# Layer 0's first shift and scale: the sums over the condition as column-packed TensorE matmuls

## The chip, the core and the metric

The kernel runs on one core of a Trainium2 chip. The core has a matrix engine (TensorE, "PE" in the profile, with its weight loads as "PEld"), a vector engine (VectorE, DVE), a scalar engine (ScalarE, ACT), GpSimd (POOL), and SyncE (SP), whose queue issues most of the DMA transfers here. TensorE writes its results into PSUM, eight banks of 128 partitions by 512 float32; everything else lies in SBUF, 128 partitions wide. Every engine works through its own queue, whose order is fixed when the kernel is built; an instruction waits there until its data have come and its buffer is free. The metric is the device time of one execution in microseconds (us); the medians of several executions are compared.

## The reference

A trunk of two layers over 256 positions of 2048 channels. What the change touches is the modulation at the head of layer 0: a condition vector `c` of 2048 elements, passed through SiLU, is multiplied with a 2048 x 12288 matrix, which gives six vectors of 2048; the first two, shift and scale, are applied to the normalised input before its projection.

```python
c_act = jax.nn.silu(c)
for l in range(DEPTH):
    mod = (c_act @ w_mod[l] + b_mod[l]).reshape(bn, 6, d)
    shift_m, scale_m, gate_m = mod[:, 0, None], mod[:, 1, None], mod[:, 2, None]
    shift_f, scale_f, gate_f = mod[:, 3, None], mod[:, 4, None], mod[:, 5, None]
    h = layer_norm(x) * (1.0 + scale_m) + shift_m
    proj = h @ w_in[l]
    ...                      # four mixers on parts of proj, concatenated
    x = layer_norm(ALPHA * x + (1.0 + gate_m) * (y @ w_out[l]), ...)
    h = layer_norm(x) * (1.0 + scale_f) + shift_f
    x = layer_norm(ALPHA * x + (1.0 + gate_f) * conv_ffn(h, ...), ...)
```

So each element of shift and scale is a dot product of 2048 terms, and all weights of the product (33.5 MB for these two vectors) are used only once.

## The kernel before

Channels are cut into 16 k-tiles of 128 (`KT`), positions into two tiles of 128. Layer 0's input projection can't start before shift and scale are there for the channels that it contracts over, so both are done in five pieces of k-tiles, `PIECES` (line 45): two, two, four, four and four k-tiles. Function `by_pieces` (in `mixers`' layer-0 case) runs over the pieces: while the products of piece q's projection run, the modulation weights of piece q+1 are loaded and summed. For every piece the projection has four parts: D (1024 columns), U, V and E (512 each), all with `mm` (line 79).

- **D** is contracted in TensorE with plain float32 operands for the first four k-tiles (`D_c<-hF,wexact` in the profile) and after that with pairs of rounded halves, `hi` and `lo`, of weights and activations (`D_c<-hT,whi`, `D_c<-hT,wlo`). The weights are split by ScalarE (line 460) and VectorE (line 461), the activations by lines 479 and 480.
- **U, V, E** are contracted with plain float32 operands (`U<-hF,wexact`, `V<-wexact,hF`, `E<-hF,wexact`). Their partial sums of a piece are copied by ScalarE out of PSUM (lines 1259 and 1264) and added by VectorE (lines 1261, 1265).

Within a piece, `by_pieces` writes the program in four steps: a quarter of D's products, then one of U, V, E; after the fourth quarter of D comes the next piece. In each step a share of the next piece's modulation units (`some_mods`) is put ahead of the products, and ahead of the last quarter of D comes `finish`, which ends the next piece's modulation and applies it to the activations `hF` (ScalarE line 82, VectorE line 1432), and from k-tile 4 on splits them into `hT`.

`mod_piece` makes the modulation of a piece. For a piece of two k-tiles a unit loads four k-rows of 128 by 256 columns of shift and 256 of scale (two DMAs of 512 KB, line 255); for a piece of four k-tiles it loads two k-rows of 128 by 512 columns of both. So a unit has always 1 MB, in one of four buffers `raw` of 128 x 2048, and pieces have 4, 4, 8, 8 and 8 units. `mod_step` (lines 238 and 240) multiplies each row of weights with the condition's element of its partition, `cact[:, kt]`, and adds it to `qacc`, on VectorE. At the end `sum_cols` sums `qacc` over the 128 partitions by small matmuls against a column of ones (`ps_mod<-ones,qacc`; each 128 columns of `qacc` are one matmul with one column of output), and `mod_cols` (lines 195 and 197) adds the bias.

PSUM: six buffers `acc` (D holds four of them through all the pieces, the other two go round among U, V and E) and two buffers `ms` for all small work. The buffers `raw` are shared with the weights of D, and later with the stream of the other modulations (`macc`, line 240), which begins with the latent projection (B) after the pieces. After the pieces the first new work of TensorE in the trace is `ps_wT` (line 952), with the products of B behind it.

Of the kernel before, what the change touches and what calls it, by code (L numbers as in the profile page):

```python
# [7 lines left out]
F32 = mybir.dt.float32  # L8
# [5 lines left out]
P = 128  # L14
D = 2048
# [3 lines left out]
KT = D // P  # L19
# [31 lines left out]
def encoder_kernel(ctx: ExitStack, tc: tile.TileContext, A: dict, consts: bass.AP, out: bass.AP):  # L51
    nc = tc.nc
    pe, act, dve, pool = nc.tensor, nc.scalar, nc.vector, nc.gpsimd

    keep = ctx.enter_context(tc.tile_pool(name="keep", bufs=1))
    rawp = ctx.enter_context(tc.tile_pool(name="rawp", bufs=4))
    splitp = ctx.enter_context(tc.tile_pool(name="splitp", bufs=4))
    tmpp = ctx.enter_context(tc.tile_pool(name="tmpp", bufs=4))
# [7 lines left out]
    def raw_tile(name):  # L66
        return rawp.tile([P, 2048], F32, tag="raw", name=name)

    def tmp_tile(name):
        return tmpp.tile([P, 512], F32, tag="tmp", name=name)  # L70

    def ms_tile(name):
        return msp.tile([P, 512], F32, tag="ms", name=name)
# [4 lines left out]
    def mm(o, lhsT, rhs, start, stop):  # L78
        pe.matmul(o, lhsT, rhs, start=start, stop=stop, skip_group_check=True)  # L79
# [19 lines left out]
    ones = ones_r.bitcast(F32)  # L99
# [21 lines left out]
    pe.transpose(pst[:, 0:16], crow[0:16, 128:256], ident[0:16, 0:16])  # L121
    cact = keep.tile([P, 16], F32, name="cact")
    dve.tensor_copy(cact, pst[:, 0:16])

    def load_rows(parts, n, dst):


        r = smallp.tile([P, P], F32, tag="rows", name="rows", bufs=4)
        at = 0
        for ap in parts:  # L130
            pool.dma_start(out=r[at : at + ap.shape[0], :], in_=ap)
            at += ap.shape[0]
        assert at == n

        def turn():
            ps = ms_tile("ps_rows")
            pe.transpose(ps[:, 0:n], r[0:n, :], ident[0:n, 0:n])
            at = 0
            for d in dst:
                dve.tensor_copy(d, ps[:, at : at + d.shape[1]])  # L140
                at += d.shape[1]

        return turn
# [44 lines left out]
    data_dep = mybir.DependencyInfo(mybir.DependencyClass.Sync, mybir.DependencyReason.DATA)  # L188

    def mod_cols(l, m, k0, ps, n):  # L190

        cols = keep.tile([P, n], F32, name=f"mod_{l}_{m}_{k0}")
        bias = bcol[l][:, m * KT + k0 : m * KT + k0 + n]
        if m in (SHIFT_M, SHIFT_F):
            done = dve.tensor_tensor(out=cols, in0=ps[:, 0:n], in1=bias, op=ALU.add)
        else:
            done = dve.scalar_tensor_tensor(
                out=cols, in0=ps[:, 0:n], scalar=1.0, in1=bias, op0=ALU.add, op1=ALU.add
            )
        for j in range(n):  # L200
            MOD[(l, m, k0 + j)] = cols[:, j : j + 1]
            MOD_BY[(l, m, k0 + j)] = done.ins.name

    def sum_cols(l, m, k0, acc):

        n = acc.shape[1] // P
        ps = ms_tile("ps_mod")
        for j in range(n):
            mm(ps[:, j : j + 1], acc[:, j * P : (j + 1) * P], ones[:, 0:1], True, True)
        mod_cols(l, m, k0, ps, n)  # L210
# [24 lines left out]
    def mod_step(acc, w, kt, first):  # L235
        col = cact[:, kt : kt + 1]
        if first:
            i = dve.tensor_scalar(out=acc, in0=w, scalar1=col, scalar2=None, op0=ALU.mult)
        else:
            i = dve.scalar_tensor_tensor(out=acc, in0=w, scalar=col, in1=acc, op0=ALU.mult, op1=ALU.add)  # L240
        held(i, "mod")

    def mod_piece(l, ms, k0, nkt):


        n, width = len(ms), nkt * P
        nk = 2048 // (n * width)
        acc = tmpp.tile([P, D], F32, tag="macc", name="qacc", bufs=2)[:, : n * width]
        units = []

        def unit(u):
            raw = raw_tile("wmod").rearrange("p (k m c) -> p k m c", k=nk, m=n)
            for i, m in enumerate(ms):
                c0 = m * D + k0 * P
                nc.sync.dma_start(
                    out=raw[:, :, i, :],
                    in_=A["w_mod"][l, u * nk * P : (u + 1) * nk * P, c0 : c0 + width].rearrange(
                        "(k p) c -> p k c", p=P
                    ),
                )  # L260
            for k in range(nk):
                mod_step(acc, raw[:, k, :, :].rearrange("p m c -> p (m c)"), u * nk + k, u == 0 and k == 0)

        for u in range(KT // nk):
            units.append(lambda u=u: unit(u))

        def sums():
            for i, m in enumerate(ms):
                sum_cols(l, m, k0, acc[:, i * width : (i + 1) * width])

        return units, sums

# [143 lines left out]
    def held(i, kind):  # L416

        name, n = hold[kind]
        if n > 0:
            hold[kind][1] = n - 1  # L420
            tc.add_manual_dep(i.ins, name, order_dep, reason="the norm is what the next products wait for")
# [990 lines left out]
    def piece(q, hF):  # L1412

        k0, nkt = PIECES[q]
        units, sums = mod_piece(0, (SHIFT_M, SCALE_M), k0, nkt)
        if q == 0:
            normed_T(hF)
            for u in units:
                u()
            turns.extend(load_params(0))  # L1420

        def finish():
            if q == 0:
                turn_b0()
            sums()
            for kt in range(k0, k0 + nkt):
                h = hF[kt // 4][:, kt % 4, :]
                sc, sh = MOD[(0, SCALE_M, kt)], MOD[(0, SHIFT_M, kt)]
                if kt % 2 == 0:
                    ident_act(h, h, sc, sh)  # L1430
                else:
                    dve.tensor_scalar(out=h, in0=h, scalar1=sc, scalar2=sh, op0=ALU.mult, op1=ALU.add)
            for kt in range(max(k0, PLAIN_KT), k0 + nkt, 2):
                split(hT[kt // 2], hF[kt // 4][:, kt % 4 : kt % 4 + 2, :])
            if q == 1:
                for turn in turns:
                    turn()
                turns.clear()

        return ([] if q == 0 else units), finish  # L1440
# [113 lines left out]
def build(inputs):  # L1554
    import numpy as np
    import concourse.bacc as bacc

    nc = bacc.Bacc("TRN2", target_bir_lowering=False, num_devices=1)
    arrays, A = {}, {}
    for name in _INS:  # L1560
        a = np.ascontiguousarray(inputs[name])
        arrays[f"in_{name}_dram"] = a
        A[name] = nc.dram_tensor(f"in_{name}_dram", a.shape, mybir.dt.from_np(a.dtype), kind="ExternalInput").ap()
    c = _constants()
    arrays["in_consts_dram"] = c
    consts = nc.dram_tensor("in_consts_dram", c.shape, F32, kind="ExternalInput").ap()
    out = nc.dram_tensor("out_0_dram", (1, S, D), F32, kind="ExternalOutput").ap()
    with tile.TileContext(nc) as tc:
        encoder_kernel(tc, A, consts, out)
    return nc, arrays  # L1570
# [8 lines left out]
```

## Time and profile before

| | us |
|---|---|
| median of 3 runs | 2282.23 (2279.7 to 2286.89) |
| profiled execution, span | 2283.6 |
| TensorE busy | 2218.9 |
| VectorE busy | 1785.1 |
| ScalarE busy | 1056.0 |

The page divides the span into 40 slices and gives each engine's busy share in tenths (9 is 90% or more), the granted TensorE clock and the DMA engines' share in the same way:

```profile
PE   5799999999999999999999999999999999999998
PEld 4687786478888888887886989877888888888886
DVE  6868899588889898998977896887776565665676
ACT  2231241354554554544556444556555554454553
POOL 1000000000000000000000000000000000000000
PEclk9999999999999999999999999999999999999999
DMA  9999879878898989988875664866765556555554
```

A slice is 57 us. The five pieces lie in the first three to four of them. A line of a group of instructions reads: line of the kernel, engine, operation, tile written and tiles read, shapes, count, then busy us and mean ns of one, then the idle time just before them with what ended it. A row of a waits view reads: who waited, for whom, us in total, times, longest us. A row of the timeline reads: start us, us, engine, line, operation, tiles and count, in brackets the idle time before it. Ends of matmuls are modelled in the profile, and a few matmul records can be missing.

### The profile page before, as it was taken

Reading aid. Unit: us, or ns where it says so; the run is one execution under the profiler, and the core shown is the slowest. Engines: PE = TensorE matmul, PEld = TensorE weight load, DVE = VectorE, ACT = ScalarE, POOL = GpSimd, SP = SyncE. Lnnn points to the kernel's source line nnn. Section 1 sums busy time; section 2 is a strip of 40 time slices with the busy share of each in tenths; the row PEclk is TensorE's granted clock in tenths of the full one; section 3 lists DMA queues with packets and bytes.
Section 4 is the critical chain, followed back from the end, with each engine's and each line's share of the span. In section 5 each row is a group of like instructions: output and inputs, shape, how many; then the busy total and the mean of one; then the engine's idle time right before and its main releaser. Section 6 shows DMA issues by size and latency. Waiting matters only on the chain. (4 is left out here: it accounts for less than half of the span.)

```text
span 2283.6 us, 29677 instructions
## 1 busy us (share of the span) xinstructions
PE 2218.9 (97%) x11502; PEld 1846.1 (81%) x11502; DVE 1785.1 (78%) x2258; ACT 1056.0 (46%) x1551; POOL 38.8 (2%) x61
## 2 busy tenths in 40 slices
PE   5799999999999999999999999999999999999998
PEld 4687786478888888887886989877888888888886
DVE  6868899588889898998977896887776565665676
ACT  2231241354554554544556444556555554454553
POOL 1000000000000000000000000000000000000000
PEclk9999999999999999999999999999999999999999
DMA  9999879878898989988875664866765556555554
GB/s 348 357 325 329 321 284 378 316 261 322 307 334 302 330 307 329 322 316 297 322 271 191 236 193 161 322 244 227 247 222 184 191 182 200 186 195 190 193 194 148
DMA packets 224565, 604.15 MB, mean 265 GB/s; under 512 B 14548, under 2 KB 27076, under 8 KB 202660
## 3 DMA queue, kind: packets, MB, share of 16 engines
q1 hardware_dynamic: 223576, 601.25, 74.2%
q8 instruction: 90, 1.47, 0.3%
q0 software_dynamic: 848, 1.01, 0.1%
q14 instruction: 51, 0.42, 0.1%
HBM read 600.11 MB, written 2.10 MB: 264 GB/s over the span
## 5 line engine op out<-in xcount | busy, mean ns | idle before, releaser
L461 DVE TENSOR_TENSOR wlo<-wraw,whi 128x1024 fp32r<-128x1024 f32 (+1 forms) x624 | 748.1, 1212 | 307.6 <-ACT whi L460 301.1
L460 ACT CAST whi<-wraw 128x1024 fp32r<-128x1024 f32 (+1 forms) x624 | 649.3, 1046 | 724.5 <-PE g_c L79 198.8
L79 PE MATMUL v_c<-hT,whi 128*128 128x512 f32 x1408 | 491.3, 393 | 0.0
L79 PE MATMUL g_c<-hT,whi 128*128 128x512 f32 x1280 | 446.8, 393 | 0.0
L79 PE MATMUL v_c<-hT,wlo 128*128 128x256 f32 x1408 | 393.9, 280 | 0.0
L79 PE MATMUL d<-whi,a 128*128 128x512 f32 x1344 | 387.7, 390 | 0.0
L240 DVE SCALAR_TENSOR_TENSOR macc<-wmod,cact,macc 128x2048 f32<-128x2048 f32 x150 | 351.7, 2344 | 19.1 <-DMA wmod<-in_w_mod_dram 18.6
L79 PE MATMUL g_c<-hT,wlo 128*128 128x256 f32 x1280 | 358.2, 280 | 0.0
L79 PEld LDWEIGHTS v_c<-hT,whi 128*128 128x128 f32 x1408 | 263.7, 187 | 59.7
L79 PEld LDWEIGHTS d<-whi,a 128*128 128x128 f32 x1344 | 252.8, 188 | 52.5
L79 PEld LDWEIGHTS g_c<-hT,whi 128*128 128x128 f32 x1280 | 239.7, 187 | 54.4
L79 PEld LDWEIGHTS v_c<-hT,wlo 128*128 128x128 f32 x1408 | 265.8, 189 | 0.2
L79 PEld LDWEIGHTS g_c<-hT,wlo 128*128 128x128 f32 x1280 | 241.7, 189 | 0.2
L79 PE MATMUL d<-wlo,a 128*128 128x512 f32 x672 | 233.8, 390 | 1.9 <-DVE wlo L461 1.9
L79 PEld LDWEIGHTS d<-wlo,a 128*128 128x128 f32 x672 | 126.6, 188 | 29.0 <-DVE wlo L461 2.7
L79 PE MATMUL o<-whi,a 128*128 128x512 f32 x352 | 101.7, 396 | 1.4 <-ACT whi L460 1.4
L872 DVE SCALAR_TENSOR_TENSOR convD<-gluD,pm,convD 128x255 f32<-128x255 f32 (+22 forms) x240 | 98.3, 460 | 0.4
L479 ACT CAST a<-g 128x512 fp32r<-128x512 f32 x132 | 81.1, 616 | 35.4 <-PE d L79 32.7
L79 PE MATMUL D_c<-hT,whi 128*128 128x256 f32 x448 | 88.0, 297 | 3.8 <-ACT hT L479 3.0
L480 DVE TENSOR_TENSOR a<-g,a 128x512 fp32r<-128x512 f32 x132 | 87.6, 683 | 1.8 <-ACT a L479 1.8
L604 PE MATMUL first<-wexact,hN 128*128 128x512 f32 x192 | 85.7, 596 | 1.5 <-ACT hN L82 1.2
L240 DVE SCALAR_TENSOR_TENSOR qacc<-wmod,cact,qacc 128x1024 f32<-128x1024 f32 (+1 forms) x75 | 80.2, 1070 | 2.4 <-DMA wmod<-in_w_mod_dram 0.4
(324 smaller groups left out, 2462.5 us busy)
## 6 DMA issues: line engine op xcount, KB each, us to landing
wraw<-in_ffn_w_up_dram SPq DMA_DIRECT2D x168, 1024.0 KB, 5.1
wmod<-in_w_mod_dram SPq DMA_DIRECT2D x160, 1024.0 KB, 6.6
wraw<-in_ffn_w_down_dram SPq DMA_DIRECT2D x88, 1024.0 KB, 5.2
wmod<-in_w_mod_dram SPq DMA_DIRECT2D x64, 512.0 KB, 8.2
wraw<-in_w_in_dram SPq DMA_DIRECT2D x30, 1024.0 KB, 7.1
wexact<-in_w_in_dram SPq DMA_DIRECT2D x52, 512.0 KB, 7.0
wraw<-in_w_out_dram SPq DMA_DIRECT2D x24, 1024.0 KB, 6.8
wexact<-in_w_out_dram SPq DMA_DIRECT2D x16, 512.0 KB, 11.8
```

The costliest lines, as they stand in the source:

```text
L79: pe.matmul(o, lhsT, rhs, start=start, stop=stop, skip_group_check=True)
L240: i = dve.scalar_tensor_tensor(out=acc, in0=w, scalar=col, in1=acc, op0=ALU.mult, op1=ALU.add)
L460: held(act.copy(hi[:, :m], r), "cast")
L461: i = dve.tensor_tensor(out=lo[:, :m], in0=r, in1=hi[:, :m].bitcast(F32), op=ALU.subtract)
L479: act.copy(hi, src)
L480: dve.tensor_tensor(out=lo, in0=src, in1=hi.bitcast(F32), op=ALU.subtract)
L604: i = pe.matmul(ps, hN[kt // 4][:, kt % 4, t * P : (t + 1) * P], parts[kt], start=kt == 0, stop=kt == KT - 1, skip_group_check=True,)
L872: dve.scalar_tensor_tensor(out=yd[:, j, 30 - k :], in0=glu[:, j, : S - 30 + k], scalar=CW(k, j), in1=yd[:, j, 30 - k :], op0=ALU.mult, op1 ...
```

## The change

The products of the modulation weights of these five pieces move from VectorE to TensorE. Every unit's 128 x 2048 of weights is cut into four stretches of 512 columns, which four matmuls stream as the moving operand. Their stationary operand is `cwide[:, kt, :]`, 128 x 32, whose first column is the condition's 128 elements of k-tile `kt` and whose other 31 columns are zero. The four outputs go to the partitions 0-31, 32-63, 64-95 and 96-127 of one PSUM bank, `ps_piece`, so that each matmul of a unit takes 32 columns of the array; the bank is summed over all the units of a piece. Only partitions 0, 32, 64 and 96 of it are not zero. A dependency makes a unit's first matmul wait for the unit's last load.

At the end of a piece ScalarE copies the bank to `prow`, and small matmuls turn it into columns: for pieces of four k-tiles, where partitions 0 and 64 hold shift (first and second k-row of a unit) and 32 and 96 hold scale, against `pick`, a 128 x 2 tile with ones where partition j belongs to shift or to scale (four matmuls of two output columns for each piece); for pieces of two k-tiles, where each stretch is one k-row with shift and scale side by side, against the ones column as before. `cwide` takes one of the two `macc` buffers.

```diff
+    cwide = tmpp.tile([P, D], F32, tag="macc", name="cwide", bufs=2)[:, 0:512].rearrange("p (k r) -> p k r", r=32)
+    pool.memset(cwide, 0.0)
+    dve.tensor_copy(cwide[:, :, 0], cact)
+    pick = keep.tile([P, 2], F32, name="pick")
+    pool.memset(pick, 0.0)
+    for j in range(4):
+        pool.memset(pick[32 * j : 32 * (j + 1), j % 2 : j % 2 + 1], 1.0)
...
         nk = 2048 // (n * width)
-        acc = tmpp.tile([P, D], F32, tag="macc", name="qacc", bufs=2)[:, : n * width]
         units = []
+        box = {}
 
         def unit(u):
+            if u == 0:
+                box["ps"] = (acc_tile if k0 == 0 else ms_tile)("ps_piece")
+            ps = box["ps"]
...
-                nc.sync.dma_start(
+                landed = nc.sync.dma_start(
...
-            for k in range(nk):
-                mod_step(acc, raw[:, k, :, :].rearrange("p m c -> p (m c)"), u * nk + k, u == 0 and k == 0)
+            flat = raw.rearrange("p k m c -> p (k m c)")
+            for j in range(4):
+                kt = u * nk + j * nk // 4
+                i = pe.matmul(
+                    ps[32 * j : 32 * (j + 1), :],
+                    cwide[:, kt, :],
+                    flat[:, j * 512 : (j + 1) * 512],
+                    start=u == 0,
+                    stop=(u + 1) * nk == KT,
+                    skip_group_check=True,
+                )
+                if j == 0:
+                    tc.add_manual_dep(i.ins, landed.ins.name, data_dep, reason="the four go side by side")
...
         def sums():
-            for i, m in enumerate(ms):
-                sum_cols(l, m, k0, acc[:, i * width : (i + 1) * width])
+            rows = tmp_tile("prow")
+            act.copy(rows, box["ps"])
+            ps = ms_tile("ps_mod")
+            if width == 512:
+                for j in range(nkt):
+                    mm(ps[:, 2 * j : 2 * j + 2], rows[:, j * P : (j + 1) * P], pick, True, True)
+                by_m = ps[:, 0 : 2 * nkt].rearrange("p (j m) -> p m j", m=2)
+                outs = [by_m[:, i, :] for i in range(n)]
+            else:
+                for i in range(n):
+                    for j in range(nkt):
+                        at = i * nkt + j
+                        mm(ps[:, at : at + 1], rows[:, at * P : (at + 1) * P], ones[:, 0:1], True, True)
+                outs = [ps[:, i * nkt : (i + 1) * nkt] for i in range(n)]
+            for o, m in zip(outs, ms):
+                mod_cols(l, m, k0, o, nkt)
```

## The prediction

> **What bounds the kernel now.** I read the page's first part, then the first 193 us, since only there does the changed code work: busy time by stretch, TensorE's waits, its timeline, VectorE's groups, the DMA queue's waits.
>
> ```profile
> span 2283.6 us, 29677 instructions
> PE 2218.9 (97%) x11502; PEld 1846.1 (81%) x11502; DVE 1785.1 (78%) x2258; ACT 1056.0 (46%) x1551; POOL 38.8 (2%) x61
> ```
>
> TensorE (PE) is busy for 97% of the span: whatever lengthens its queue lengthens the kernel, unless it falls into one of its 65 us of gaps. The sum below is made against this execution's span, 2283.6 us; the median of the runs, 2282.23 us, is 1.4 us less, and the difference found is put on the median.
>
> ```profile
> 0.00:32.90 32.90, 9.02 (x42) 7.11 (x42) 20.97 (x40) 10.08 (x15) 8.09 (x22) 0.94 0.98 331
> 32.90:84.40 51.50, 42.10 (x172) 32.28 (x172) 38.91 (x51) 11.14 (x19) 6.05 (x12) 0.93 1.00 359
> 84.40:193.00 108.60, 105.42 (x560) 87.80 (x561) 79.17 (x80) 23.31 (x33) 0.00 (x0) 0.96 0.94 341
> ```
>
> Columns: stretch, length, busy PE, weight loads, VectorE, ScalarE, GpSimd, granted clock, DMA share, GB/s. Up to 84.4 us the DMA engines are full (0.98 and 1.00 of their time), and PE has gaps: 9.4 us of 51.5. From 84.4 to 193 PE is the bound: 105.4 of 108.6 us.
>
> ```profile
> PE ps_mod L79 <- DVE qacc L240: 5.3, 2, 4.7
> PE E L79 <- DMA wexact<-in_w_in_dram: 3.1, 1, 3.1
> PE D_c L79 <- ACT hT L479: 3.0, 1, 3.0
> PE V L79 <- DMA wexact<-in_w_in_dram: 2.7, 1, 2.7
> PE D_c L79 <- DVE wlo L461: 2.4, 2, 1.8
> ...
> SPq L255 <- DVE qacc L240: 49.6, 20, 9.7
> ...
> 101.09 7.88 DVE L240 SCALAR_TENSOR_TENSOR qacc<-wmod,cact,qacc 128x1024 f32<-128x1024 f32 x6
> 108.89 1.22 DVE L461 TENSOR_TENSOR wlo<-wraw,whi 128x1024 fp32r<-128x1024 f32 x1
> ```
>
> So VectorE's products (qacc) cost PE 5.3 us of waits, most of it before the first projection, and the 2.4 us for wlo, since wlo stands behind six of them in VectorE's queue (the last two rows). The row of the DMA queue (SPq) shows loads of modulation weights waiting for VectorE to free buffers; with the DMA engines full all the same, that wait costs little.
>
> **What goes.**
>
> ```profile
> L240 DVE SCALAR_TENSOR_TENSOR qacc<-wmod,cact,qacc 128x1024 f32<-128x1024 f32 (+1 forms) x75 | 80.2, 1070 | 2.4 <-DMA wmod<-in_w_mod_dram 0.4
> L238 DVE TENSOR_SCALAR qacc<-wmod,cact 128x1024 f32<-128x1024 f32 (+1 forms) x5 | 3.2, 644 | 0.6 <-DMA wmod<-in_w_mod_dram 0.6
> 149.34 2.60 DVE L240 SCALAR_TENSOR_TENSOR qacc<-wmod,cact,qacc 128x1024 f32<-128x1024 f32 x2
> ...
> wmod<-in_w_mod_dram SPq DMA_DIRECT2D x64, 512.0 KB, 8.2
> ```
>
> VectorE loses all 80 products, 83.4 us, the last of which end at 152 us. It is not the bound of the stage, so this is worth only the waits above. The 64 loads of these weights (last row) stay as they are.
>
> **What comes.** There are 4+4+8+8+8 = 32 units of four matmuls, each 128x32 weights against 512 float32 columns: 128 matmuls. No row has a 32-column one. The nearest are V's, also float32 with 512 columns:
>
> ```profile
> 92.75 7.07 PE L79 MATMUL U<-hF,wexact 128*128 128x256 f32 x32
> 99.90 7.03 PE L79 MATMUL V<-wexact,hF 128*128 128x512 f32 x16
> 101.19 0.19 PEld L79 LDWEIGHTS V<-wexact,hF 128*128 128x128 f32 x1 [0.24 <-issue]
> 101.62 0.19 PEld L79 LDWEIGHTS V<-wexact,hF 128*128 128x128 f32 x1 [0.24 <-issue]
> ```
>
> The code has 4 k-tiles x 2 token tiles = 8 matmuls there, the trace 16 records: a float32 matmul is two passes, each with its own weight load, T = 0.43 us apart, 0.86 us in all. Time goes with the streamed columns (U's records, 256 columns, take half: 7.07/32 = 0.22 us); that 31 of the 32 weight columns are zero saves nothing by itself. All rests on u, the time of a unit of four:
>
> - All four at once: 2T = 0.86 us.
> - One after the other: 8T = 3.44 us.
> - In between: the queue holds first pass, second pass, first pass, second pass. Both passes of a matmul use the same 32 columns and cannot overlap. If starts keep the queue's order, the second matmul's first pass starts only beside the first one's second pass: each matmul adds T, the last one T more. That is 5T = 2.15 us for a unit alone, 4T = 1.72 us for units that follow each other.
>
> I take the third, in the middle of its two ends, u = 1.94: it needs nothing but the order that V's records show. The other two are the ends of the range.
>
> [...]
>
> [...]
>
> **The sums and the chain behind them.**
>
> ```profile
> L79 PE MATMUL ps_mod<-ones,qacc 128*128 128x1 f32 x56 | 6.6, 246 | 0.6 <-DVE qacc L240 0.6
> 30.16 1.84 PE L79 MATMUL ps_mod<-ones,qacc 128*128 128x1 f32 x8 [4.66 <-DVE qacc L240]
> 32.94 6.77 PE L79 MATMUL D_c<-hF,wexact 128*128 128x256 f32 x16 [0.94 <-ACT hF L82]
> 52.48 0.95 PE L79 MATMUL ps_mod<-ones,qacc 128*128 128x1 f32 x8
> 79.46 1.95 PE L79 MATMUL ps_mod<-ones,qacc 128*128 128x1 f32 x16 [0.64 <-DVE qacc L240]
> 84.43 1.46 PE L79 MATMUL D_c<-hT,whi 128*128 128x256 f32 x4 [3.03 <-ACT hT L479]
> 156.67 1.84 PE L79 MATMUL ps_mod<-ones,qacc 128*128 128x1 f32 x16
> 193.01 0.60 PE L952 MATMUL ps_wT<-cst,gmlp 128*128 128x128 f32 x4
> L1264 ACT COPY part<-U 128x512 f32<-128x512 f32 x6 | 3.5, 586 | 36.1 <-PE U L79 36.1
> ```
>
> Pieces 0 and 1 keep 4 sums (8 records); pieces 2 to 4 have 4 instead of 8, about 0.95 us less each. New ahead of them is a ScalarE copy of 128x512, 0.59 us by the nearest copy, five times, behind whatever else is in ScalarE's queue. ScalarE is busy 34.5 of 160 us here, so I add no more than the copy and 0.3 us of handover. The memsets (GpSimd, 8 us busy of the first 33) and the strided copy into cwide lie under the loads of x. ps_piece holds one of the two small PSUM buffers through pieces 1 to 4; what takes turns in the other (the sums, four parameter transposes) waits at most for its copies, below 2 us in all, inside u's spread.
>
> **The start.** The loads ahead of piece 0's last are x (2.1 MB), piece 0 (4.2) and constants (0.6): 6.9 MB at 331 GB/s is 21 us, say 22. A unit (1.9), copy and handover (0.9), then from sums to first projection as before, 32.94-30.16 = 2.8: first projection at 28 us, not 32.9. Earlier units run in PE's gap while loads come in.
>
> ```profile
> 26.91 3.10 DVE L240 SCALAR_TENSOR_TENSOR qacc<-wmod,cact,qacc 128x512 f32<-128x512 f32 x4
> 32.90:36.40 3.50, 3.46 (x8) 2.81 (x9) 3.32 (x6) 0.00 (x0) 0.00 (x0) 0.50 1.09 356
> 84.40:90.00 5.60, 5.57 (x25) 5.40 (x26) 5.53 (x7) 0.50 (x1) 0.00 (x0) 0.50 0.84 276
> 110.10:114.10 4.00, 3.94 (x21) 3.94 (x22) 3.96 (x6) 0.00 (x0) 0.00 (x0) 0.59 1.04 403
> ```
>
> The first row is what goes there: VectorE finished piece 0 at 30.0. The others show PE at half clock behind each gap, which costs 1.75, 2.8 and 1.6 us.
>
> **The sum.** First part: 28 + 42.1 busy - 1.75 (clock; PE has now been at work) - 1.0 (piece 2's sums) + 12u (pieces 1 and 2, 4 + 8 units, which stand in PE's queue among the first two pieces' projections) + 3.0 (wait for hT, kept) = 70.35 + 12u, where before it was 84.43. Second part: 108.6 - 1.6 (the clock dip behind the wlo gap) - 2.4 (wlo, now without qacc ahead) - 1.9 (sums of pieces 3 and 4) + 16u (their units) = 102.7 + 16u. The stage ends at 173 + 28u instead of 193.0. With u = 1.94 this is 227.3, **34 us later**: 2282.2 + 34.3 = 2316 us. Behind 193 us PE's order is the same and it stays the bound, so the delay lasts to the end.
>
> A unit's first matmul now waits in PE's queue for a 1 MB load, and all projections behind it wait with it. Up to the end of piece 2's weights 24.7 MB have to come in (the 6.9 above, pieces 1 and 2 with 12.6, projection weights of two pieces with 5.2), 71.6 us at 345 GB/s, the mean of the first two stretches; with 12u = 23 PE gets there later than the data, so that wait adds nothing in the forecast.
>
> **Rivals.**
>
> *Full packing.* If the four go entirely side by side, u = 0.86: the end is 173 + 24.1 = 197.1, +4 us, 2286. If the wait for hT is covered as well (projections are left over at that point) and its clock dip with it, 5.4 us less: 2281. So between 2280 and 2288: not slower by what can be told. For it: the code makes the four ready together. Against it: V's two records for each matmul, if starts keep the queue's order. [...]
>
> *Full packing and a gain behind the stage.* VectorE, rid of 83 us, enters the next stages with less left over.
>
> ```profile
> 220.00:240.00 20.00, 17.60 (x67) 11.57 (x66) 18.46 (x36) 5.50 (x20) 3.84 (x3) 1.00 0.96 324
> 240.00:260.00 20.00, 19.79 (x83) 16.11 (x84) 17.18 (x32) 2.43 (x6) 0.00 (x0) 0.91 0.62 224
> 280.00:300.00 20.00, 18.63 (x94) 16.15 (x94) 19.95 (x41) 2.58 (x9) 0.00 (x0) 1.00 0.85 319
> ```
>
> In these three stretches VectorE is nearly full and PE loses 2.4 + 0.2 + 1.4 us and about 1.8 us of clock (0.09 of 20): at most 5.8 us are to be had, and 2281 becomes 2275, just faster. Against it: the products removed end at 152 us, 68 us before the first of these stretches, and the load of the stretches themselves is unchanged.
>
> *No overlap.* u = 3.44: the end is 269.3, +76, 2358. This is the case that the change doesn't do what it says. For it: every record of this trace runs behind the one before it. Against it: the four write different rows of the bank and hold different columns of the array.
>
> *Loads decide.* PE reaches each unit before its load, and the projections queued behind a unit wait with it. It decides where PE would be ready for piece 2's first projection before 71.6 + 3 (chain) = 74.6 us; by 70.35 + 12u that is so only below u = 0.4, and the lowest case has 0.86. It gets no chance of its own.
>
> **How the numbers follow.** Passes overlapping in queue order: 0.52, with its own range from u = 1.72 to 2.42 (173 + 28u: 221 to 241), 2310 to 2330. Full packing, the stage alone: 0.18, of which 0.13 within 0.3% of before and the rest slower. Full packing with the later gain: 0.15, faster. No overlap: 0.15, slower. About 0.3%, 6.8 us, is what a measurement of this kernel can tell from no change. So faster 0.15, same 0.13, slower 0.72. The range goes from 2270 to 2345: it holds the first three cases with some room at both ends, and leaves out the fourth with a remainder of 0.05.
>
> **What would show it.** Each step in the changed profile: units of four writing ps_piece with their records 0.43 us apart and pairs sharing a start (forecast), all eight within 0.9 us (packing), or eight in 3.4 us (no overlap); no qacc on VectorE and about 83 us less in its sum; the first D_c at about 28 us instead of 32.9; the first D_c from hT, after piece 2, at about 94 us instead of 84.4; ps_wT at about 227 us instead of 193; PE without waits for loads between. The forecast falls if u is below 1.2 or above 2.6, or if ps_wT moves and the end does not.

## The result, and the profile after

The changed kernel takes 2308.75 us (median of 4 runs, 2306.06 to 2309.03), the kernel before 2283.41 (median of 4, 2279.7 to 2286.89): 1.0099 times as long, 95% interval 1.0085 to 1.0113. That is 23 us more by this ratio and 25 by the medians: slower by about 1%, clear of the noise. The profiled execution has a span of 2306.7 us.

The page of the changed kernel, first part:

```profile
span 2306.7 us, 30068 instructions
PE 2256.8 (98%) x11734; PEld 1843.7 (80%) x11734; DVE 1704.8 (74%) x2179; ACT 1057.7 (46%) x1556; POOL 39.5 (2%) x67
```

VectorE is busy for 80 us less, TensorE for 38 us more, and the span is 23 us longer: whatever VectorE's relief bought, it is less than what TensorE's load cost. Where that cost came through is seen at three places of TensorE's timeline. Of the changed kernel:

```profile
29.63 6.75 PE L79 MATMUL D_c<-hF,wexact 128*128 128x256 f32 x16 [1.01 <-ACT hF L82]
...
85.76 1.07 PE L274 MATMUL ps_piece<-wmod,cwide 128*32 128x512 f32 x8
88.31 1.43 PE L79 MATMUL D_c<-hT,whi 128*128 128x256 f32 x5 [1.49 <-ACT hT L514]
...
209.77 0.60 PE L987 MATMUL ps_wT<-cst,gmlp 128*128 128x128 f32 x4
```

The first projection starts 3.3 us sooner than before (29.6 against 32.9), piece 2's first D product 3.9 us later (88.3 against 84.4), and the stage ends 16.8 us later (209.8 against 193.0). So the loss grows piece by piece. The last 6 us of the difference arise behind the stage, where TensorE's matmuls are the same in both traces, 10728 in the same order of tiles; the experiments come back to that.

One unit of the changed kernel, first TensorE's matmuls in its timeline:

```profile
41.82 1.06 PE L274 MATMUL ps_piece<-wmod,cwide 128*32 128x512 f32 x8
42.81 0.48 PE L79 MATMUL D_c<-hF,wexact 128*128 128x256 f32 x1
```

Its weight loads in the timeline:

```profile
41.81 0.16 PEld L274 LDWEIGHTS ps_piece<-wmod,cwide 128*32 128x32 f32 x8 [0.33 <-issue]
```

And ps_piece alone in stretches of 0.05 us (length, busy time and matmuls in progress, busy time and weight loads, then ScalarE's copy, clock, DMA share, GB/s):

```profile
41.83:41.88 0.05, 0.05 (x4) 0.05 (x8) 0.00 (x0) 1.00 1.39 533
...
42.18:42.23 0.05, 0.05 (x4) 0.00 (x0) 0.00 (x0) 1.00 0.51 205
...
42.28:42.33 0.05, 0.05 (x8) 0.00 (x0) 0.00 (x0) 1.00 1.75 696
...
42.53:42.58 0.05, 0.05 (x4) 0.00 (x0) 0.00 (x0) 1.00 0.73 287
...
42.93:42.98 0.05, 0.00 (x0) 0.00 (x0) 0.00 (x0) 1.00 1.66 656
```

(128*32 is the tile of the array: 128 rows, 32 columns.) All eight weight loads are done in 0.16 us. Then four records are in progress from the first stretch on, the other four join at about 42.25 us, 0.43 us later, while the modelled ends of the first four run out, and at 42.81 the next product starts. So a unit takes 0.99 us, not 1.94. The records don't name the pass; but a single matmul's two records run one behind the other (0.98 us in the run without the dependency, below), so the four that start together are read as the first passes of all four matmuls, and the next four as their second passes.

TensorE's waits from 26 to 210 us, from just ahead of the first sums to the end of the stage, after:

```profile
PE ps_mod L79 <- ACT prow L290: 2.4, 2, 1.8
PE D_c L79 <- ACT whi L495: 1.5, 2, 0.8
PE D_c L79 <- ACT hT L514: 1.5, 1, 1.5
PE D_c L79 <- ACT hF L82: 1.0, 1, 1.0
```

No wait for a load is left, neither for projection weights (5.8 us before) nor for the modulation's, and none for VectorE. New is the wait for the copy prow. With the busy times of the two stages the difference can be added up. Of the changed kernel, stretch from the first D_c to ps_wT, all instructions, ps_piece alone and ps_mod alone:

```profile
29.63:209.77 180.14, 175.22 (x933) 118.65 (x933) 48.17 (x66) 36.46 (x55) 5.95 (x12) 0.96 0.90 315
...
29.63:209.77 180.14, 30.08 (x224) 4.76 (x224) 2.38 (x4) 0.96 0.90 315
...
29.63:209.77 180.14, 4.08 (x32) 3.95 (x32) 0.92 (x8) 0.96 0.90 315
```

And of the kernel before, the same two ends, all instructions and ps_mod alone:

```profile
32.94:193.01 160.07, 147.53 (x732) 120.09 (x733) 118.05 (x130) 34.47 (x51) 6.05 (x12) 0.95 0.96 347
...
32.94:193.01 160.07, 6.58 (x56) 6.80 (x56) 1.27 (x8) 0.95 0.96 347
```

The stretch is 20.1 us longer: 28 units with 30.1 us of busy time (1.07 each, with modelled ends that reach into the next product), sums 2.5 less, idle time 7.6 less (12.5 to 4.9). 30.1 - 2.5 - 7.6 = 20.0. With the start 3.3 us sooner, 16.8.

### The profile page after: what moved, and what is told of

Its sections match the earlier page's. It is cut to its first block, busy times and chain, and to the rows that moved or that the text cites. A ratio compares the mean times of both kernels' runs of the same rounds, so it can differ in the third digit from the quotient of the medians.

```text
span 2306.7 us, 30068 instructions
## 1 busy us (share of the span) xinstructions
PE 2256.8 (98%) x11734; PEld 1843.7 (80%) x11734; DVE 1704.8 (74%) x2179; ACT 1057.7 (46%) x1556; POOL 39.5 (2%) x67
## 5 line engine op out<-in xcount | busy, mean ns | idle before, releaser
L79 PEld LDWEIGHTS o<-whi,a 128*128 128x128 f32 x352 | 68.1, 194 | 16.9 <-ACT whi L495 2.6
```

## The experiments

All are compared with the kernel before on the same chip. "At the first out-projection" is the start of the first matmul of `o`, the first of layer 0's output projection; it is a better mark than ps_wT, which in some kernels is queued earlier.

**Each unit's products twice** (label e_double). The condition in `cwide` is halved, so that the sums are the same.

```diff
-    dve.tensor_copy(cwide[:, :, 0], cact)
+    dve.tensor_scalar(out=cwide[:, :, 0], in0=cact, scalar1=0.5, scalar2=None, op0=ALU.mult)
...
-            for j in range(4):
+            for r, j in enumerate((0, 1, 2, 3, 0, 1, 2, 3)):
                 kt = u * nk + j * nk // 4
...
-                    start=u == 0,
-                    stop=(u + 1) * nk == KT,
+                    start=u == 0 and r < 4,
+                    stop=(u + 1) * nk == KT and r >= 4,
```

> The changed kernel with each unit's four products issued twice (condition halved), so 128 more column-packed matmuls and nothing else. Theory (the units' TensorE time is what the change costs): 28 units behind the first projection cost their time in full, about 1.0 us each, the four ahead of it little: 2309 + 25 to 32 = 2334 to 2341 us. Rival (the change costs by its waits, for loads, for the copy out of PSUM or for the small PSUM buffers, and TensorE has room): below 2320 us. If a second group of four can't start beside or close behind the first, a unit takes over 2.2 us and the time goes above 2341.

2323.13 us, 1.0170 (1.0153 to 1.0188): 14 us more than the changed kernel, between the two expectations and outside both. The profile of this kernel says why. Its ps_piece group (busy, mean ns of one), and below it that of the changed kernel:

```profile
L274 PE MATMUL ps_piece<-wmod,cwide 128*32 128x512 f32 x512 | 64.0, 619 | 10.8 <-DVE rs_in L668 10.8
```

```profile
L274 PE MATMUL ps_piece<-wmod,cwide 128*32 128x512 f32 x256 | 37.8, 634 | 10.7 <-DVE rs_in L668 10.5 <-DMA wmod<-in_w_mod_dram 0.3
```

TensorE's waits of this kernel over the same time, and its busy times in the stretch to 209.77 us:

```profile
PE D_c L79 <- ACT hF L82: 1.0, 1, 1.0
PE ps_mod L79 <- ACT prow L290: 0.5, 1, 0.5
```

```profile
32.10:209.77 177.67, 177.67 (x1074) 110.56 (x1075) 47.87 (x63) 36.41 (x54) 5.93 (x12) 0.99 0.87 307
```

TensorE is busy for 26.2 us more on ps_piece, 23.5 of them behind the first projection, which itself starts 2.5 us later (32.1 against 29.6). But its waits fall from 6.4 to 1.5 us, and with no gap left the clock stays up, 0.99 instead of 0.96. From the first projection to the first out-projection TensorE is idle for 3.0 us less, and all its other products take 7.1 us less (271.0 instead of 278.1), at a clock of 0.99 instead of 0.97. 2.5 + 23.5 - 3.0 - 7.1 = 15.9, and the first out-projection starts that much later, 362.2 against 346.3 us. So the theory missed its range, and its mechanism holds with a correction: the changed kernel had 10 us of slack left, idle time and the half clock behind it (0.50 from 88.0 to 93.8 us, behind the wait of 1.5 us for hT), and the next us of product time goes into that first. The waits of the change are not what it costs.

**No column packing** (label e_serial): 128 stationary columns of which one is not zero, all four into the whole bank.

```diff
-    cwide = tmpp.tile([P, D], F32, tag="macc", name="cwide", bufs=2)[:, 0:512].rearrange("p (k r) -> p k r", r=32)
+    cwide = tmpp.tile([P, D], F32, tag="macc", name="cwide", bufs=2)
...
-    dve.tensor_copy(cwide[:, :, 0], cact)
+    dve.tensor_copy(cwide.rearrange("p (k r) -> p k r", r=P)[:, :, 32], cact)
...
-                    ps[32 * j : 32 * (j + 1), :],
-                    cwide[:, kt, :],
+                    ps,
+                    cwide[:, kt * P + 32 - 32 * j : (kt + 1) * P + 32 - 32 * j],
                     flat[:, j * 512 : (j + 1) * 512],
-                    start=u == 0,
-                    stop=(u + 1) * nk == KT,
+                    start=u == 0 and j == 0,
+                    stop=(u + 1) * nk == KT and j == 3,
```

> The changed kernel without column packing: the same four products for each unit, one after the other, each with 128 stationary columns of which one is not zero, into all 128 partitions of the same bank. Theory (packing is complete: four cost about as much as one): a unit goes from 1.0 to 3.4 us, 28 units behind the first projection add 28 x 2.4 = 68 us, with the first four up to 75: 2375 to 2385 us. Rival (packing saves only half, as the prediction has it, u = 1.94): 28 x 1.5 = 42 us, 2351 us.

2368.66 us (one run), 60 us more than the changed kernel, nearer to the theory but short of it. Its ps_piece group, then three units in a row of its timeline:

```profile
L274 PE MATMUL ps_piece<-wmod,cwide 128*128 128x512 f32 x256 | 115.8, 600 | 11.0 <-DMA wmod<-in_w_mod_dram 11.0
```

```profile
69.20 10.46 PE L274 MATMUL ps_piece<-wmod,cwide 128*128 128x512 f32 x24
79.50 1.89 PE L79 MATMUL D_c<-hF,wexact 128*128 128x256 f32 x8
```

24 records from 69.20 to 79.50 are 0.43 us each, 3.4 us for a unit. Busy time on ps_piece is 78 us more than packed (75 expected); 60.4 us of it arrive at the first out-projection (406.7 against 346.3). The slack just found is taken here too: of waits in the stage 0.6 us are left, and the granted clock from 29.6 to 236 us is 1.00. So not packing costs 2.4 us for each unit in TensorE's time, which is what packing saves; it is one execution, without an interval.

**No dependency on the last load** (label e_nodep). The order built then queues other products between a unit's first matmul and the other three.

```diff
-                if j == 0:
...
-                    tc.add_manual_dep(i.ins, landed.ins.name, data_dep, reason="the four go side by side")
```

> The changed kernel without the dependency that makes a unit's first product wait for its last load. The order built then puts other products between the first and the other three of some units. Theory (products run side by side only with those next to them in the queue): a unit cut in two pays a second pair of passes, 0.9 us; with about half of the 28 units cut, 10 to 16 us more, 2319 to 2325 us. Rival (TensorE packs across what lies between, or the cut is made up by shorter waits for loads): within 3 us of the changed kernel, 2306 to 2312 us.

2324.85 us, 1.0172 (1.0154 to 1.0189), 16 us more than the changed kernel, as the theory said. Of the 28 units behind the first projection 16 are cut in two, and ps_piece is busy for 55.3 instead of 37.8 us. One of them, in the timeline:

```profile
72.18 1.04 PE L274 MATMUL ps_piece<-wmod,cwide 128*32 128x512 f32 x2
73.16 0.70 PE L79 MATMUL D_c<-hF,wexact 128*128 128x256 f32 x2
73.79 1.06 PE L274 MATMUL ps_piece<-wmod,cwide 128*32 128x512 f32 x6
74.78 0.48 PE L79 MATMUL D_c<-hF,wexact 128*128 128x256 f32 x1
```

One matmul (two records) takes 0.98 us until the next product, three take 0.99, four in the changed kernel 0.99. So here the matmuls went side by side only with those next to them in the queue, and the dependency, which might seem a needless wait, is worth 16 us here.

**Only some pieces on TensorE** (labels e_p0, e_p01, e_p012). `mod_piece` takes the old way (products on VectorE, `sum_cols`) for the other pieces; `ON_PE` holds the pieces' first columns and is (0, 2) in e_p01 and (0, 2, 4) in e_p012.

```diff
+ON_PE = (0,)
...
     def mod_piece(l, ms, k0, nkt):
+        if k0 not in ON_PE:
+            return mod_piece_dve(l, ms, k0, nkt)
```

> Only piece 0's products go to TensorE; pieces 1 to 4 stay on VectorE as before. Theory (the change pays where TensorE has a gap, and costs a unit's time wherever it has none): the first projection starts 3 us earlier (29.6 instead of 32.9 us) and no unit stands behind it; if what comes next follows, 2280 us, 3 us less than before. Rival (loads and VectorE set when piece 2 is ready, whatever piece 0 does): the first 3 us are lost again before the first D_c from hT at 84.4 us, and the time is that of before within 1 us.

> Pieces 0 and 1 on TensorE, 2 to 4 on VectorE. Theory: piece 1's four units stand among piece 0's projections and cost 4 us; 3 us from the start and up to 3 us of the waits for loads before 84 us come back: 2280 to 2285 us. Rival (each unit behind the first projection is paid in full and nothing comes back): 2287 us.

> Pieces 0 to 2 on TensorE, 3 and 4 on VectorE. Theory: the first D_c from hT comes as in the changed kernel, at 88.3 us, 3.9 us later than before, and behind it VectorE has room for the products and TensorE none, so the rest is as before but for 2 to 4 us of waits: 2285 to 2289 us; the other 16 units make the remaining 20 us of the change. Rival (the loss is not in pieces 3 and 4 above all): over 2297 us.

| on TensorE | median us | ratio to before (95%) | first D_c from hT | first out-projection |
|---|---|---|---|---|
| none (before) | 2284.93 | 1 | 84.4 | 329.8 |
| piece 0 | 2286.59 | 1.0010 (1.0000 to 1.0020) | 81.3 | 324.4 |
| pieces 0, 1 | 2292.11 | 1.0030 (1.0019 to 1.0041) | 85.0 | 332.4 |
| pieces 0 to 2 | 2294.06 | 1.0042 (1.0029 to 1.0055) | 84.6 | 333.6 |
| all (the change; its own before is 2283.41) | 2308.75 | 1.0099 (1.0085 to 1.0113) | 88.3 | 346.3 |

The two places come from one profile of each kernel; the three profiles of before that the next experiment has differ there by up to 1.6 and 3.2 us. With piece 0 alone the head start is kept, 3.1 us at piece 2 and 5.4 at the first out-projection, as the theory said; in the medians nothing of it is left, where 3 us had been expected, so the rival was wrong on the place and right on the sum. Pieces 0 and 1 missed the expectation: the median is 7 us above the theory's range and 5 above the rival. At piece 2 the four units of piece 1 show as 3.7 us (81.3 to 85.0), near their time of 4 x 0.99, though 1.4 us of it is a later first projection in this profile (30.4 against 29.0). At the first out-projection only 2.6 us against before are left; most of the miss lies behind the stage. For pieces 0 to 2 piece 2 starts sooner than expected (84.6), the median is 2294 where 2285 to 2289 was expected: by the medians about two fifths of the loss (9 of 23 us) come with 16 of the 32 units, by the first out-projection 3.8 of 16.5 us. The 16 units of pieces 3 and 4, where TensorE had been busy for 105.4 of 108.6 us, make 12.7 us at that place (333.6 to 346.3).

**Where the last 6 us come from** (labels e_before, e_before2, e_after2, e_p0_2, e_afterb, e_p0b). Behind the first out-projection the first profile of before has 1953.8 us left, that of the changed kernel 1960.4. Most of that is in layer 1's FFN products, where TensorE's same queue runs at two paces. (`g_c` and `v_c` are the two halves of the FFN's first projection, `first` is the first 512 columns of it, `ps_gT` their transposes.) Of the kernel before and of the changed one, matmuls of g_c in a row:

```profile
1604.65 0.39 PE L79 MATMUL g_c<-hT,whi 128*128 128x512 f32 x1
1604.88 0.28 PE L79 MATMUL g_c<-hT,wlo 128*128 128x256 f32 x1
1604.99 0.39 PE L79 MATMUL g_c<-hT,whi 128*128 128x512 f32 x1
...
1608.81 0.39 PE L79 MATMUL g_c<-hT,whi 128*128 128x512 f32 x1
```

```profile
1623.72 0.40 PE L79 MATMUL g_c<-hT,whi 128*128 128x512 f32 x1
1623.95 0.28 PE L79 MATMUL g_c<-hT,wlo 128*128 128x256 f32 x1
1624.07 0.40 PE L79 MATMUL g_c<-hT,whi 128*128 128x512 f32 x1
...
1627.96 0.40 PE L79 MATMUL g_c<-hT,whi 128*128 128x512 f32 x1
```

Twelve pairs take 4.16 us before and 4.24 after, 1.9% more, without a gap and at the same granted clock of 1.00, for 250 us on end. Two new kernels (e_afterb, e_p0b) and four repeats of earlier ones asked what sets this. In e_afterb and e_p0b prow lies in the unused part of cwide's buffer:

```diff
-    cwide = tmpp.tile([P, D], F32, tag="macc", name="cwide", bufs=2)[:, 0:512].rearrange("p (k r) -> p k r", r=32)
+    cwhole = tmpp.tile([P, D], F32, tag="macc", name="cwide", bufs=2)
+    cwide = cwhole[:, 0:512].rearrange("p (k r) -> p k r", r=32)
...
-            rows = tmp_tile("prow")
+            rows = cwhole[:, 512:1024]
```

> The kernel before, profiled once more. The two profiles so far differ by 16.8 us at the first matmul behind the five pieces (193.0 against 209.8 us) and by 6.3 us more behind it, where the code is the same. Theory: the 6.3 us are of this one execution (stretches of 100 to 200 us in which TensorE starts 134 to 135 records in 23.5 us instead of 137 to 138) and no effect of the change; then the length behind ps_wT, 2090.6 us in the first profile, comes out differently here by several us. Rival: it belongs to the change; then 2090 to 2091 us again.

> The changed kernel with the copy of the sums (prow) put in the unused rest of cwide's buffer, so that the buffers tmp are handed out later as in the kernel before. Asked: why TensorE, with the same queue behind the pieces, takes 473.5 us from the last first-tile transpose to the last v_c in layer 1, where both profiles of before have 469.0. Theory: prow's five turns shift which tmp buffers the FFN uses, and that sets the pace; then 469.0 here and about 6 us less than the changed kernel, 2303 us. Rival: something else of the change or of the execution; then 473.5 and 2307 to 2310 us.

> Piece 0 alone on TensorE, prow in cwide's buffer. Theory as for the other run: with the pace of before behind the pieces the 5.4 us that the first such kernel had gained at the first out-projection (324.4 against 329.8 us) last to the end: 2279 to 2281 us, faster than before by 0.2%. Rival: the pace stays at 473.5, and the time is that of before, 2284 to 2287 us.

> The kernel before, profiled a third time, for TensorE's pace behind the pieces: from the last first-tile transpose (ps_gT) to the last v_c of layer 1 both profiles so far show 467.3 us. Theory (the pace belongs to the built program): 467.3 within 0.3. Rival (it differs by execution): anything up to 472.

> The changed kernel, profiled a second time. Theory (the pace belongs to the built program): 471.8 us from the last ps_gT to the last v_c of layer 1, as in its first profile, with the slow stretch over the first 250 us. Rival (it differs by execution): another length, 467 to 471, and then the 6.3 us behind the pieces are no part of the change.

> Piece 0 alone on TensorE, a second profile. Theory (built program): 471.9 us as in its first profile, and the first out-projection again 5 us before that of the kernel before, at 324 to 325 us. Rival (by execution): 467 to 471.

From the last ps_gT to the last v_c (the expectations that say 469.0 and 473.5 count from the last matmul of `first`, 1.7 us sooner):

| kernel | from ps_gT to v_c, us | left behind the first out-projection, us |
|---|---|---|
| before, three profiles | 467.3, 467.3, 467.4 | 1953.8, 1955.6, 1951.9 |
| changed, two profiles | 471.8, 471.9 | 1960.4, 1961.3 |
| changed, prow moved | 471.8 | 1957.9 |
| products doubled; not packed; no dependency | 471.8; 471.8; 471.8 | 1958.7; 1960.1; 1959.8 |
| piece 0, two profiles | 471.9, 468.3 | 1960.4, 1954.4 |
| piece 0, prow moved | 468.4 | 1954.9 |
| pieces 0, 1; pieces 0 to 2 | 471.9; 468.3 | 1959.5; 1955.9 |

Medians: the copy of before 2286.07 (1.0002, 0.9990 to 1.0014); the changed kernel with prow moved 2304.23 (1.0091, 1.0074 to 1.0108), not to be told from the changed kernel; piece 0 with prow moved 2282.59 (1.0000, 0.9990 to 1.0010). The single executions profiled once more took 2282.37 (before), 2307.3 (changed) and 2281.55 us (piece 0).

The theory of the buffers fell: with prow moved the changed kernel has the slow pace still, and piece 0 with prow moved, whose median lies between its two expectations, has the pace that piece 0 showed once without the move. The first repeat of before took 4.1 us longer behind ps_wT than its first profile (2094.7 against 2090.6), as the theory of a chance execution asked, but at the same pace of 467.3. One built program, piece 0 alone, had both paces in two executions, so the pace is not a property of the program alone. Yet before had the fast one in all three profiles, and all six profiles of kernels with all five pieces on TensorE had the slow one. That ties the slow pace to the change without a mechanism. What sets it stays open, and with it how far these 6 to 7 us belong to the change; the stage itself accounts for 16.5 us between the two first profiles and for 15 by the means of all (first out-projection at 328.7 to 331.9 us before, 344.1 and 346.3 after).

No version beat the kernel before by what can be told; piece 0 alone is level with it.

## Why the prediction was right or wrong

The direction was right, and the time came out near the forecast (2316 forecast, 2308.75 measured; 34 us of loss forecast, 23 to 25 measured). But the main term was wrong, and that the sum is near is luck: 24 us too much for the units were partly made up by 7 us too little within the stage and 6 us behind it that the sum did not have. By the prediction's own sign, u below 1.2, its account falls.

- **The step that failed is u**, "If starts keep the queue's order, the second matmul's first pass starts only beside the first one's second pass". The trace shows four records together and the other four behind them, read above as all first passes and then all second ones: 0.99 us for a unit alone, 1.07 us of busy time, where 1.94 was taken. That is 28 x 0.87 = 24 us too much. The row on which it rested, two records for each of V's matmuls (16 for 8, 0.43 us apart), says that a matmul has two passes; it doesn't say in which order the passes of several matmuls run, and nothing else in the trace did.
- A group of four lasted about as long as one matmul: 0.99 us in the changed kernel against 0.98 for a single one of 32 columns in the run without the dependency. Of the three values that the prediction set out for u, that is nearest to the first, 0.86.
- **The rival with the right mechanism had the wrong time.** Full packing gave 2280 to 2288. It lacked the changeover between full-width and 32-column products (0.99 us to the next product against 0.86, 0.13 us for each of 25 rows of units, 3 us, for which its sum has no term), one unit at half clock (1.87 us, at a clock of 0.50 from 88.0 to 93.8 us), and what the next points name.
- The forecast's own range goes up to u = 2.42, 0.27 us above the 2.15 of a unit alone: no run shows these 0.27 us for each unit. The runs showed 0.13 us for each row of units in their place (0.99 against 0.86).
- The first projection: 28 us forecast, 29.6 measured, again at half clock (0.50 from 29.6 to 32.9 us), where 1.75 us had been taken off for a full clock.
- Piece 2's first D product: with u = 1.07 the prediction's 70.35 + 12u is 83.2; measured 88.3. Of the 5.1 us, 1.6 are the start, 1.7 the clock, 1.1 a unit of piece 3 that stands ahead of it in the queue, and the chain through prow waits 3.3 us in two places (1.8 for the copy, 1.5 for hT) instead of 3.0; 0.4 us are left over.
- The second part: 102.7 + 15 units is 118.8 us; 121.5 were measured, 2.7 more: 1.5 us of new waits for whi came in place of the 2.4 that did vanish for wlo, and 1.2 us are not accounted for.
- "Loads decide" was rightly given no chance: behind the first products no matmul of a unit waits for its load. The waits for projection weights, 5.8 us before, vanished, as the sum had taken without saying so: its first part adds only busy time and the wait for hT.
- VectorE's 80 us less bought nothing that shows but those waits. The rival that had it help in the next stages found nothing: from ps_wT to the first out-projection the two first profiles take 136.8 us before and 136.5 after, and the rest is longer, not shorter.
- "Behind 193 us PE's order is the same" holds, but the conclusion that the time there is the same does not: 6 to 7 us were added, open as told.

So the changed kernel is slower, for the 15 to 17 us of the stage, because its products moved from an engine with room to the one that sets the stage's length. That is shown by the added-up busy times, by the doubled products, and by pieces 3 and 4. For the 6 to 7 us behind the stage no cause is shown.

## What to carry to other kernels

Work that moves onto the engine that bounds a stage is paid there, less only what its gaps take, even with its products packed four at a time: here 30 us of products made the stage's stretch 20 us longer. First look which engine has room in which stretch, not over the whole kernel. Where that engine has gaps with a slow clock behind them (0.50 here from 88.0 to 93.8 us), the first few us of new work go into these gaps: here 26 us more of products cost 16. If column-packed matmuls are used, keep the members of a group next to each other in the queue; one matmul cut off cost as much here as the whole group (0.98 us against 0.99).

## What the runs showed of the hardware

- Four float32 matmuls of 128 rows by 32 columns and 512 streamed columns took 0.99 us as one group between full-width products and 5.29 us as six groups in a row (48 records of the run with doubled products, below): 0.86 us for each further group, as much as a single matmul of 128 columns (0.86). One of 32 columns between full-width products took 0.98 us. Packing is worth a factor of 3.9 within the row of six (3.43 against 0.88).

```profile
61.18 5.36 PE L274 MATMUL ps_piece<-wmod,cwide 128*32 128x512 f32 x48
66.47 1.99 PE L79 MATMUL D_c<-hF,wexact 128*128 128x256 f32 x8
```

- The changeover between the two widths thus cost about 0.13 us at each row of groups (0.99 against 0.86). No row shows what it consists of.
- The same queue of TensorE ran 1.9% slower for up to 250 us on end, at a granted clock of 1.00 and without a wait in the trace (12 pairs in 4.24 instead of 4.16 us). It was not expected, and what sets it was not found.
